# Writing down TensorE's order in the scan stage of a hybrid S5, attention and FFN step, and moving eight modulation products into it

## The chip, the cores and the metric

One NeuronCore of one Trainium2 chip runs the whole step as one program. The metric is the device time of one execution in microseconds; smaller is better. The kernel before was run three times and profiled once.

## What is computed

One layer is applied with the same weights to 128 context tokens and to 128 latent tokens (model width 2048), so that every weight matrix is multiplied with 256 token columns. Cut to what matters here:

```python
mod = silu(cond) @ w_mod + b_mod          # 12288 columns: shift1 scale1 gate1 shift2 scale2 gate2
xm  = rmsnorm(x) * (1 + scale1) + shift1
u, q, k, v, g_s, g_a = split(xm @ w_in)   # 1024, 1024, 256, 256, 2048, 2048 columns
# branch S: per group of 16 channels a 64-dim complex diagonal recurrence, forwards and backwards
h = scan(lam_bar, b_bar @ u, h0)          # one for each of the two directions
y = u * d + real(C @ h)                   # both directions added
z = gelu(y);  z = z * sigmoid(z @ w_glu)
# branch A: grouped-query attention with a sink logit
merged = sigmoid(g_s) * (z @ w_ssm_o) + sigmoid(g_a) * (attention @ w_attn_o)
x  = x + gate1 * (merged @ w_out)
xm2 = rmsnorm(x) * (1 + scale2) + shift2
x  = x + gate2 * ((silu(conv(xm2 @ w_up)_a) * conv(xm2 @ w_up)_b) @ w_down)
```

All data are fp32. The large products are made in three matmuls on a split of each operand into a rounded high part and the low rest (lo·hi, hi·lo and hi·hi); the small ones run in plain fp32.

## The kernel before

**Loads.** Weights come from DRAM in tiles of 512 KB (two rows of 128, 512 columns), one DMA each, issued by SyncE (SP) in the order of the program. They land in the pool `raw`, which has five buffers (`RAW = 5`). There are two kinds of users. A *weight chunk* of a large product is split: ScalarE (ACT) rounds it to `hi` (line 184), VectorE (DVE) takes the rest `lo` (line 185), and then its raw buffer is free; TensorE (PE) runs 24 matmuls of 128x256 on it. The split is written two chunks ahead of its use and has a raised priority. A *modulation pair* is two raw tiles which PE reads directly in one burst of four fp32 matmuls (the trace has eight rows for it, line 263); both buffers are free only when the burst has run. `burst` keeps a pair together.

**The scan stage.** The 64 groups are worked off in eight quarters `q`. For each quarter PE multiplies the channels with the input matrix (`bu_mm`, 16 fp32 matmuls), DVE rotates the result (`rot_in`, twice), runs the two scans (`scans`) and rotates back (`rot_out`, twice), and PE adds up the output (`yout`: 7 matmuls on the channels and 64 on the states), which ACT passes through gelu. Beside this stand `m_gen` (16 matmuls for the taps inside a block of four tokens), the products that prepare the matrices of a later quarter on DVE (`b_prod`, `c_prod`, `tables`), their copies on ACT, and 16 transposes on PE (`b_exp`). Transposes, the attention and the convolution's rows share one PSUM buffer, `misc`, so each user of it waits until the copy of the one before is made.

**What fills it.** While the chain of a quarter waits, PE works on 56 weight chunks (attention gate, attention output, SSM gate: the list `fill`) and on 48 modulation bursts (`modfill`, column groups 8 to 19). `weave` spreads the two lists evenly between the steps of the scan. That is the order of the program only: the framework's scheduler decides the order on each engine, by priority and its own estimate of when operands are there, and may take an instruction ahead of earlier ones. The attention's last softmaxes stand just ahead of the scan stage in the program.

**The up projection.** Column groups 20 to 23 of `w_mod` (gate2) are multiplied later: four bursts while the second norm is made, and twelve between the weight chunks of the first third of the up projection.

Of the kernel before, what the change touches and what calls it, by code (L numbers as in the profile page):

```python
# [97 lines left out]
def tile_hybrid_step(ctx, tc, a):  # L98
# [35 lines left out]
    steps = []  # L134
# [161 lines left out]
    def mod_steps(gs, pool="raw"):  # L296
        nb = len(gs)
        st = {}

        def chunk(b, ku):  # L300
            def f(raw):
                if ku % 2 == 0:
                    st["r"] = raw
                    return
                if b == 0 and ku == 1:
                    st["a"] = PS([128, 512], "mod")
                prev = None
                for i, r in ((ku, raw), (ku - 1, st["r"])):
                    for j in range(2):
                        with tc.issue_after(prev.ins) if prev is not None else nullcontext():  # L310
                            prev = mod_mm(st["a"], 2 * i + j, r[:, j, :], b, b == 0 and i < 2, b + 1 == nb and i > 5)
                if b + 1 == nb and ku == 7:
                    one = all(g == gs[0] + i for i, g in enumerate(gs))
                    mod_pp(st["a"], nb, [(4 * gs[0], 0, 4, 0, nb)] if one else [(4 * g, 0, 4, i, 1) for i, g in enumerate(gs)])
            return f
        return [Step(chunk(b, ku), wsrc(a["w_mod"], 2 * ku, 512 * MOD_AT[g]), False, pool, frees=2 * (ku % 2)) for b, g in enumerate(gs) for ku in range(8)]
# [364 lines left out]
    def weave(main, *fills):  # L681
        n = len(main)
        pos = [0] * len(fills)
        for i, s_ in enumerate(main):
            steps.append(s_)
            for k, fl in enumerate(fills):
                fl, lo, hi = fl if isinstance(fl, tuple) else (fl, 0.0, 1.0)
                while pos[k] < len(fl) and pos[k] * (hi - lo) * n < (i + 1 - lo * n) * len(fl):
                    end = burst(fl, pos[k])
                    steps.extend(fl[pos[k]:end])  # L690
                    pos[k] = end
        for k, fl in enumerate(fills):
            steps.extend((fl[0] if isinstance(fl, tuple) else fl)[pos[k]:])
# [33 lines left out]
    modfill = []  # L727
    for i in range(8, 20, 4):
        modfill += mod_steps(list(range(i, i + 4)))
    weave(ssm.stages(), (fill, FF0, FF1), (modfill, MF0, MF1))  # L730
    for i in range(NGS, 4):
        steps.extend(gs(i))

# [242 lines left out]
            gfb.append(t)  # L976

    CUT = [0, 8, 15, 22]
    g2s = mod_steps([20, 21, 22, 23])
    for x in g2s[:G2B]:  # L980
        x.pool = "first"

# [63 lines left out]
def SSM(nc, a, T4, S4, T2, PS, hp, ident, i32r, dvec, uT):  # L1046
# [241 lines left out]
    def b_prod(qd, ri):  # L1288
        if ri == 0:
            G["tB"] = S4([128, 2, 4, 8, 16], "tB")  # L1290
            G["BL"] = []
        prod(G["tB"][:, ri], "B", G["LB"], qd, 0, ri, 1, 1 - ri, OP.add if ri else OP.subtract)

    def b_exp(qd, d):
        BD, tB = G["BD"], G["tB"]
        for h in range(2):
            hs = slice(64 * h, 64 * h + 64)
            for ri in range(2):
                src = tB[hs, ri].rearrange("p k (q d) c -> p d q k c", d=2)[:, d]
                ACT(BD[hs, ri, :, :, h, :], src if d else src[:, :, ::-1, :], AF.Copy)  # L1300
                if d == 0:
                    ACT(G["B0"][hs, ri, :, h, :], tB[hs, ri, 0], AF.Copy)
        BL = S4([128, 2, 4, 128], "BL")
        G["BL"].append(BL)
        for ri in range(2):
            p = PS([128, 4, 128], "misc")
            for q in range(4):
                TR(p[:, q, :], BD[:, ri, q].rearrange("p e g c -> p (e g c)"), ident)
            ACT(BL[:, ri], p, AF.Copy)

    def u_exp(qd):
        G["U4", qd] = hp.tile([128, 4, 64], F32, tag="U4", name="U4", bufs=2)
# [133 lines left out]
    def s(f, *x):  # L1446
        return Step(lambda: f(*x))

    def b_side(q):
        if q > 7:  # L1450
            return []
        return [s(b_prod, q, 0), s(b_prod, q, 1), s(b_exp, q, 0), s(tables, q), s(b_exp, q, 1)]

    def c_side(q):
        return [s(c_prod, q, 0), s(c_prod, q, 1)] if q < 8 else []

    def first():
        return b_side(0) + c_side(0) + [s(decay, 0)]

    def stages():  # L1460
        st = [s(u_exp, 0), s(u_exp, 1), s(c_exp, 0), s(bu_mm, 0), s(rot_in, 0, 0), s(m_gen, 0), s(rot_in, 0, 1)] + b_side(1) + c_side(1)
        for q in range(8):
            st += [s(scans, q), s(rot_out, q, 0), s(rot_out, q, 1)]
            if q < 7:
                st += [s(decay, q + 1), s(bu_mm, q + 1)]
            if q < 6:
                st += [s(u_exp, q + 2)]
            st += [s(yout, q)]
            if q < 7:
                n = [s(c_exp, q + 1), s(rot_in, q + 1, 0), s(rot_in, q + 1, 1), s(m_gen, q + 1)]  # L1470
                b_, c_ = b_side(q + 2), c_side(q + 2)
                st += n[:2] + b_[:1] + n[2:3] + b_[1:2] + n[3:] + b_[2:] + c_
        st.append(Step(finals))
        return st
    S.first = first
    S.stages = stages
    return S
# [26 lines left out]
```

## Time and profile before

| | us |
|---|---|
| median of three runs | 1551.19 (1549.31 to 1555.21) |
| profiled execution | 1552.15 |
| its span in the trace | 1550.1 |
| PE busy | 1491.0 (96% of the span) |
| PE weight loads busy | 1311.1 (85%) |
| DVE busy | 1007.7 (65%) |
| ACT busy | 766.7 (49%) |

The trace covers the span; the remaining 2 us lie around it. PE's busy time counts each matmul with its modelled tail, so that a stretch in which PE waits little after each matmul looks fuller than it is. Times inside the trace are counted from the span's start.

### The profile page before, as it was taken

How to read it: one execution, taken by the hardware profiler on the slowest of the kernel's cores; microseconds unless marked ns; L12 is line 12 of the kernel's file. 1: busy time of each engine (PE TensorE's matmuls, PEld its weight loads, DVE VectorE, ACT ScalarE, POOL GpSimd, SP SyncE). 2: the span in 40 equal slices, each digit the busy share in tenths (PEclk: the TensorE clock that was granted, in tenths of full speed). 3: DMA queues.
4: the chain of work that ended last, by engine and by line, in shares of the span. 5: the costliest groups of instructions: out<-in, count | busy, mean ns of one | idle time of the engine just before them, and what ended most of it. 6: DMA issues, size and time to landing. Idle time of an engine off the chain costs nothing.

```text
span 1550.1 us, 29294 instructions
## 1 busy us (share of the span) xinstructions
PE 1491.0 (96%) x11871; PEld 1311.1 (85%) x11871; DVE 1007.7 (65%) x1541; ACT 766.7 (49%) x1191; POOL 85.7 (6%) x179
## 2 busy tenths in 40 slices
PE   6989999999899999999999999999999999999997
PEld 5758799778677788998689999889999988999986
DVE  4997776468866566765665656655665655666665
ACT  6335537645545666544554544433544543545543
POOL 2000004022321000000000000000000000000000
PEclk9999999999999999999999999999999999999999
DMA  9999754774676677975566676765555565566563
GB/s 352 352 340 321 286 196 157 258 277 156 209 241 238 240 250 274 310 244 192 172 242 235 205 245 201 238 200 190 176 192 181 181 197 191 175 205 197 170 203 123
DMA packets 104246, 349.18 MB, mean 225 GB/s; under 512 B 13900, under 2 KB 16628, under 8 KB 104112
## 3 DMA queue, kind: packets, MB, share of 16 engines
q1 hardware_dynamic: 98576, 344.20, 64.9%
q0 software_dynamic: 5312, 3.05, 0.8%
q8 instruction: 93, 1.52, 0.4%
q14 instruction: 41, 0.34, 0.1%
q10 hardware_dynamic: 224, 0.08, 0.0%
HBM read 343.76 MB, written 2.46 MB: 223 GB/s over the span
## 4 chain that ended last, share of the span: by engine, by line
PE 83%; DMA 8%; DVE 4%; ACT 2%; issue 1%; POOL 1%; SPq 0%; DVEq 0%; ACTq 0%
PE acc L395 16%; PE acc L396 16%; PE acc L397 16%; PE acc L421 8%; PE acc L422 8%; PE acc L423 8%; PE mod L263 5%; DMA raw<-in_w_mod_dram 2%; DMA raw<-in_w_in_dram 2%; PE bu L1375 1%; DVE lo L185 1%; DMA rw<-in_w_mod_dram 1%; DMA U<-u 1%; DMA raw<-in_w_attn_o_dram 1%; ACT hi L184 1%
## 5 line engine op out<-in xcount | busy, mean ns | idle before, releaser
L185 DVE TENSOR_TENSOR lo<-raw,hi 128x1024 fp32r<-128x1024 f32 (+1 forms) x456 | 538.7, 1186 | 444.8 <-ACT hi L184 442.8
L184 ACT ACTIVATE hi<-raw 128x1024 fp32r<-128x1024 f32 (+1 forms) x456 | 468.5, 1029 | 609.1 <-PE acc L397 260.7
L395 PE MATMUL acc<-yh,lo 128*128 128x256 f32 x1408 | 400.0, 284 | 0.0
L396 PE MATMUL acc<-yl,hi 128*128 128x256 f32 x1408 | 398.8, 283 | 0.0
L397 PE MATMUL acc<-yh,hi 128*128 128x256 f32 x1408 | 398.7, 283 | 0.0
L395 PEld LDWEIGHTS acc<-yh,lo 128*128 128x128 f32 x1408 | 270.3, 192 | 8.9 <-DVE lo L185 4.2
L396 PEld LDWEIGHTS acc<-yl,hi 128*128 128x128 f32 x1408 | 270.3, 192 | 0.1
L397 PEld LDWEIGHTS acc<-yh,hi 128*128 128x128 f32 x1408 | 270.2, 192 | 0.0
L395 PE MATMUL acc<-xh,lo 128*128 128x256 f32 x568 | 166.8, 294 | 9.3 <-ACT sig L672 4.8
L396 PE MATMUL acc<-xl,hi 128*128 128x256 f32 x568 | 163.4, 288 | 0.0
L397 PE MATMUL acc<-xh,hi 128*128 128x256 f32 x568 | 163.1, 287 | 0.0
L422 PE MATMUL acc<-lo,ff 128*128 128x512 f32 x352 | 136.8, 389 | 0.0
L423 PE MATMUL acc<-hi,ff 128*128 128x512 f32 x352 | 136.8, 389 | 0.0
L395 PEld LDWEIGHTS acc<-xh,lo 128*128 128x128 f32 x568 | 109.2, 192 | 31.4 <-DVE lo L185 6.9
L421 PE MATMUL acc<-hi,ff 128*128 128x512 f32 x352 | 127.8, 390 | 0.0
L396 PEld LDWEIGHTS acc<-xl,hi 128*128 128x128 f32 x568 | 109.6, 193 | 2.4 <-issue 2.2
L397 PEld LDWEIGHTS acc<-xh,hi 128*128 128x128 f32 x568 | 109.5, 193 | 0.7 <-issue 0.7
L263 PE MATMUL mod<-raw,cst 128*32 128x512 f32 x480 | 72.2, 631 | 8.0 <-DMA raw<-in_w_mod_dram 7.2
L421 PEld LDWEIGHTS acc<-hi,ff 128*128 128x128 f32 x352 | 66.1, 188 | 14.7 <-issue 1.1
L423 PEld LDWEIGHTS acc<-hi,ff 128*128 128x128 f32 x352 | 66.1, 188 | 13.7
L422 PEld LDWEIGHTS acc<-lo,ff 128*128 128x128 f32 x352 | 66.1, 188 | 13.5
L1316 POOL DMA_DIRECT2D U<-u x128 | 62.6, 497 | 159.6 <-PE bu L1375 138.5
(365 smaller groups left out, 2149.3 us busy)
## 6 DMA issues: line engine op xcount, KB each, us to landing
raw<-in_w_up_dram SPq DMA_DIRECT2D x176, 512.0 KB, 4.2
raw<-in_w_mod_dram SPq DMA_DIRECT2D x120, 512.0 KB, 5.1
raw<-in_w_in_dram SPq DMA_DIRECT2D x88, 512.0 KB, 4.5
raw<-in_w_down_dram SPq DMA_DIRECT2D x88, 512.0 KB, 4.3
rw<-in_w_mod_dram SPq DMA_DIRECT2D x56, 512.0 KB, 6.6
raw<-in_w_out_dram SPq DMA_DIRECT2D x32, 512.0 KB, 4.1
rw<-in_w_mod_first_dram SPq DMA_DIRECT2D x16, 512.0 KB, 7.4
raw<-in_w_in_dram SPq DMA_DIRECT2D x32, 256.0 KB, 6.1
```

The lines of the kernel that those rows point to most:

```text
L184: ACT(th[:, w], raws[n][:, w], AF.Copy)
L185: TT(tl[:, w], raws[n][:, w], f32(th[:, w]), OP.subtract)
L263: return MM(acc[32 * j:32 * j + 32], cst[:, kt, 6 - 2 * b:38 - 2 * b], rhs, start=start, stop=stop, skip_group_check=True, tile_position=( ...
L395: MM(o, wl, xh, start=start, stop=False, skip_group_check=True)
L396: MM(o, wh, xl, start=False, stop=False, skip_group_check=True)
L397: MM(o, wh, xh, start=False, stop=stop, skip_group_check=True)
L421: MM(accs[s], xl, hi[:, j, :], start=(kt == first), stop=False)
L422: MM(accs[s], xh, lo[:, j, :], start=False, stop=False)
L423: lastmm[0] = MM(accs[s], xh, hi[:, j, :], start=False, stop=(kt == last - 1))
L1316: nc.gpsimd.dma_start(G["U4", qd][32 * e:32 * e + 32, q, :], u[32 * q:32 * q + 32, 64 * e:64 * e + 64])
L1375: MM(bu[:, ri, x], BL[d][:, ri, q, :], u[:, :, ::-1] if d else u, start=(x == 0), stop=True, skip_group_check=True)
```

## The change

The scan stage's part of PE is put into a region in which PE keeps the order of the program (`manual_schedule`); the other engines are scheduled as before. The stage's steps are written as a period that is the same for every quarter, with places marked `F` (one weight chunk) and `M` (one modulation burst): seven `F` and six `M` for a quarter. `b_exp` is cut into its copies (`b_bd`) and its transposes (`b_tr`), and several steps stand elsewhere in the period. Column groups 20 and 21 join `modfill`, so that 56 bursts are spread over 48 places `M`; the up projection keeps groups 22 and 23.

```diff
-    weave(ssm.stages(), (fill, FF0, FF1), (modfill, MF0, MF1))
+    modfill += mod_steps([20, 21])
+    plan = ssm.stages()
+    region = ExitStack()
+    step(lambda: region.enter_context(tc.manual_schedule(engines={mybir.EngineType.PE})))
+    left = {"fill": [[u] for u in fill], "mod": []}
+    while modfill:
+        end = burst(modfill, 0)
+        left["mod"].append(modfill[:end])
+        modfill = modfill[end:]
+    share = {k: (len(v), plan.count(k)) for k, v in left.items()}
+    seen = dict.fromkeys(left, 0)
+    for x in plan:
+        if x in left:
+            seen[x] += 1
+            n, m = share[x]
+            for _ in range(n * seen[x] // m - n * (seen[x] - 1) // m):
+                steps.extend(left[x].pop(0))
+        else:
+            steps.append(x)
+    step(region.close)
+    steps.append(ssm.finals())
...
-    g2s = mod_steps([20, 21, 22, 23])
+    g2s = mod_steps([22, 23])
...
     def stages():
-        st = [s(u_exp, 0), s(u_exp, 1), s(c_exp, 0), s(bu_mm, 0), s(rot_in, 0, 0), s(m_gen, 0), s(rot_in, 0, 1)] + b_side(1) + c_side(1)
+        F, M = "fill", "mod"
+        st = [s(u_exp, 0), s(u_exp, 1), s(c_exp, 0)] + b_side(1)
         for q in range(8):
...
+            n = q + 1
+            more = n < 8
+            st += [s(bu_mm, q), s(rot_in, q, 0), M, s(rot_in, q, 1), F, s(scans, q)]
+            st += [s(decay, n)] if more else []
+            st += [M, s(m_gen, q), F, s(rot_out, q, 0), M]
+            st += [s(b_bd, n, 0)] if more else []
+            st += [s(rot_out, q, 1), F]
+            st += [s(tables, n), s(b_tr, n, 0, 0), M, s(b_tr, n, 0, 1), F] if more else [M, F]
+            st += ([s(b_bd, n, 1)] if more else []) + c_side(n) + [F]
+            st += [s(b_tr, n, 1, 0), M, s(b_tr, n, 1, 1), F] if more else [M, F]
+            st += b_side(n + 1) + [s(yout, q)]
+            st += [s(c_exp, n)] if more else []
+            st += [s(u_exp, q + 2)] if q < 6 else []
+            st += [F, M]
```

The changed kernel's instructions can be listed in the order in which each engine gets them. At the end of the attention PE had, before, the last score matmuls (L625) and the first half of an attention output (L658) with weight chunks (L395 to L397) between them, taken from the scan stage's fill:

```order
L625 MATMUL bu<-kT,pg 128x128 x3
L658 MATMUL misc<-P,pg 128x512
L658 MATMUL misc<-P,kT 128x512
L625 MATMUL bu<-kT,pg 128x128
L396 MATMUL acc<-xl,hi 128x256
L397 MATMUL acc<-xh,hi 128x256
L395 MATMUL acc<-xh,lo 128x256
```

The changed kernel has there, in one go, the transposes of probabilities (L651), the attention outputs (L658) and the first transposes for the scan (L1330, `b_tr`):

```order
L651 MATMUL misc<-kc,P 128x128 x4
L625 MATMUL bu<-kT,pg 128x128 x4
L658 MATMUL misc<-P,pg 128x512
L658 MATMUL misc<-P,kT 128x512
L625 MATMUL bu<-kT,pg 128x128 x4
L651 MATMUL misc<-kc,P 128x128 x4
L658 MATMUL misc<-P,pg 128x512
L651 MATMUL misc<-kc,P 128x128 x8
L658 MATMUL misc<-P,pg 128x512
L658 MATMUL misc<-P,kT 128x512
L1330 MATMUL misc<-kc,BD 128x128 x8
```

What PE does for the scan stage's fill can no longer move ahead of the region, so nothing stands between these any more.

On SP, the queue of the loads, this is the border of two quarters in the changed kernel (`raw<-in_w_mod_dram` x2 is one modulation pair, a row of another matrix is a weight chunk):

```order
L155 DMA raw<-in_w_mod_dram 128x1024 x2
L155 DMA raw<-in_w_in_dram 128x1024 x2
L155 DMA raw<-in_w_mod_dram 128x1024 x6
L155 DMA raw<-in_w_in_dram 128x1024
L155 DMA raw<-in_w_mod_dram 128x1024 x2
L155 DMA raw<-in_w_attn_o_dram 128x1024
```

Before, pairs and chunks alternated over the whole stage:

```order
L155 DMA raw<-in_w_mod_dram 128x1024 x2
L155 DMA raw<-in_w_attn_o_dram 128x1024
L155 DMA raw<-in_w_mod_dram 128x1024 x2
L155 DMA raw<-in_w_attn_o_dram 128x1024 x2
L155 DMA raw<-in_w_mod_dram 128x1024 x2
L155 DMA raw<-in_w_attn_o_dram 128x1024
```

The places `M` at the end of a quarter get two bursts, and with the first of the next quarter three pairs follow each other.

On DVE a quarter of the changed kernel begins like this (L185 splits a weight chunk, L1410 to L1413 are `rot_in`, L1419 the scans, L1427 to L1429 `rot_out`):

```order
L185 TENSOR_TENSOR lo<-raw,hi 128x1024
L1410 TENSOR_TENSOR vv<-bu,tab 128x512
L1412 TENSOR_TENSOR vv<-vv,t_4921 128x512
L185 TENSOR_TENSOR lo<-raw,hi 128x1024
L1413 TENSOR_TENSOR vv<-vv,keep 128x8
L1419 SCALAR_TENSOR_TENSOR vv<-R,vv 128x512 x2
L1427 TENSOR_TENSOR H<-vv,tab 128x16x32
L1429 TENSOR_TENSOR H<-H,t_5041 128x16x32
L185 TENSOR_TENSOR lo<-raw,hi 128x1024
```

The rows that repeat are left out: between the first split and the second stand six large operations of `rot_in`, between the scans and the third split five of `rot_out`. The first split is that of the first chunk of the quarter, the second and third those of the next two.

## Rows read from the trace of the kernel before

**Rows 1.** The page: busy time of each engine, share of the span, instructions.
```profile
PE 1491.0 (96%) x11871; PEld 1311.1 (85%) x11871; DVE 1007.7 (65%) x1541; ACT 766.7 (49%) x1191; POOL 85.7 (6%) x179
```

**Rows 2.** Stretches: length, busy PE, PEld, DVE, ACT, POOL, PE's clock, DMA share, GB/s.
```profile
350.00:400.00 50.00, 44.05 (x613) 36.57 (x611) 44.37 (x80) 32.48 (x79) 15.63 (x32) 0.93 0.38 130
400.00:450.00 50.00, 48.28 (x512) 38.47 (x513) 35.41 (x55) 25.51 (x53) 7.83 (x16) 1.00 0.77 261
610.00:700.00 90.00, 90.00 (x667) 86.23 (x666) 59.25 (x68) 45.34 (x52) 0.99 (x2) 1.00 0.82 282
850.00:900.00 50.00, 50.00 (x414) 47.09 (x413) 29.18 (x36) 23.54 (x29) 0.00 (x0) 1.00 0.68 238
```

**Rows 3.** SP's waits in the scan stage: total us, times, longest.
```profile
SPq L155 <- PE mod L263: 101.2, 33, 18.4
```

**Rows 4.** PE in order of time where the two orders part, and where the stage ends.
```profile
259.77 1.04 PE L263 MATMUL mod<-raw,cst 128*32 128x512 f32 x2
...
608.62 0.36 PE L395 MATMUL acc<-zh,lo 128*128 128x256 f32 x1
```

**Rows 5.** ACT and DVE in order of time at the attention's end.
```profile
265.70 0.61 ACT L652 ACTIVATE P<-misc 128x512 f32<-128x512 f32 x1
...
278.47 1.28 ACT L638 ACT_TABLE_LOAD   x1 [1.85 <-DVE st L633]
...
282.27 0.40 ACT L638 ACTIVATE P<-bu,st 128x128 f32<-128x128 f32 x1
...
286.59 1.25 ACT L1328 ACTIVATE CL<-bct 64x128 f32<-64x128 f32 x4
...
303.13 0.83 ACT L1300 ACTIVATE BD<-tB 64x256 f32<-64x256 f32 x2
...
297.96 0.69 DVE L664 TENSOR_TENSOR ol<-misc,oh 128x512 fp32r<-128x512 f32 x1
```

**Rows 6.** The chain that ended last: start, length of the piece, engine, tile, line, count.
```profile
294.34 1.72 PE misc L658 x4
...
316.93 0.12 PE acc L397
...
319.21 0.44 PE misc L1308 x4
319.65 1.73 PE bu L1375 x16
...
342.56 1.51 PE y L1416 x14
...
520.14 0.73 PE y L1338 x32
...
546.27 1.94 PE y L1425 x128
```

**Rows 7.** The same chain around two loads that a finished modulation burst let start.
```profile
308.45 1.02 PE mod L263 x8
309.47 4.14 DMA raw<-in_w_attn_o_dram
...
314.79 1.24 DVE lo L185
316.07 0.39 PE acc L395
...
396.63 0.29 SPq L155
396.97 4.28 DMA raw<-in_w_attn_o_dram
```

**Rows 8.** The chain again, on DVE: one large operation of `rot_in`, one scan.
```profile
386.68 0.60 DVE t L1389
...
392.18 1.11 DVE vv L1397
```

**Rows 9.** The chain in the up projection: one modulation burst.
```profile
831.85 1.00 PE mod L263 x8
```

More of the change, by code (lines that the diff above doesn't have):

```diff
@@ L1290, in b_prod, with b_bd @@
             G["tB"] = S4([128, 2, 4, 8, 16], "tB")
-            G["BL"] = []
         prod(G["tB"][:, ri], "B", G["LB"], qd, 0, ri, 1, 1 - ri, OP.add if ri else OP.subtract)
-    def b_exp(qd, d):
+    def b_bd(qd, d):
         BD, tB = G["BD"], G["tB"]
@@ L1302, in b_exp, with b_tr @@
                     ACT(G["B0"][hs, ri, :, h, :], tB[hs, ri, 0], AF.Copy)
[L1303 to L1309, printed above, removed]
+    def b_tr(qd, d, ri):
+        if (d, ri) == (0, 0):
+            G["BL"] = []
+        if ri == 0:
+            G["BL"].append(S4([128, 2, 4, 128], "BL"))
+        p = PS([128, 4, 128], "misc")
+        for q in range(4):
+            TR(p[:, q, :], G["BD"][:, ri, q].rearrange("p e g c -> p (e g c)"), ident)
+        ACT(G["BL"][d][:, ri], p, AF.Copy)
     def u_exp(qd):
@@ L1447, in s, with b_side @@
         return Step(lambda: f(*x))
[L1449 to L1452, printed above, removed]
     def c_side(q):
         return [s(c_prod, q, 0), s(c_prod, q, 1)] if q < 8 else []
+    def b_side(q):
+        return [s(b_prod, q, 0), s(b_prod, q, 1)] if q < 8 else []
     def first():
-        return b_side(0) + c_side(0) + [s(decay, 0)]
+        n = b_side(0) + [s(b_bd, 0, 0), s(b_tr, 0, 0, 0), s(b_tr, 0, 0, 1), s(tables, 0), s(b_bd, 0, 1), s(b_tr, 0, 1, 0), s(b_tr, 0, 1, 1)]
+        return n + c_side(0) + [s(decay, 0)]
     def stages():
-        st = [s(u_exp, 0), s(u_exp, 1), s(c_exp, 0), s(bu_mm, 0), s(rot_in, 0, 0), s(m_gen, 0), s(rot_in, 0, 1)] + b_side(1) + c_side(1)
+        F, M = "fill", "mod"
+        st = [s(u_exp, 0), s(u_exp, 1), s(c_exp, 0)] + b_side(1)
         for q in range(8):
[L1463 to L1473, printed above, removed]
+            n = q + 1
[12 more added lines that the diff above has]
+            st += [F, M]
         return st
+    S.finals = lambda: s(finals)
     S.first = first
```

## The prediction

> **What bounds the kernel now.** The page comes first: PE is busy for 96% of the span, every other engine far less [rows 1]. So time is saved only where PE waits, or where PE gets less work. The view by stretches shows where that is: after the scan stage PE has no gap at all (90.00 of 90 us, 50.00 of 50 us in the up projection), while in the scan stage it lost 5.95 us of one stretch of 50 us and 1.72 us of the next [rows 2]. These are lower bounds, since a busy PE includes the tails of matmuls. Counting work by prices is stricter. The chain gives them: 0.12 us for a matmul of a weight chunk, so 2.87 us for its 24; 0.44 us for four transposes; 1.73 us for 16 rows of `bu_mm`, which has 32, so 3.45; 1.51 for `yout`'s product with the channels, 1.94 for its product with the states, 0.73 for `m_gen` [rows 6], and 1.0 us for a modulation burst [rows 7]. A quarter with seven chunks and six bursts is then 20.1 + 6.0 + 3.45 + 0.73 + 1.76 + 1.51 + 1.94 = 35.5 us of PE work, eight of them 284 us. With 12 us for the attention's remainder and an earlier chunk, PE had some 296 us to do between the place where the two orders part, 259.8, and the first matmul of the gated unit at 608.6 [rows 4]. That stretch took 348.8 us, so PE lost about 53 us in it.
>
> What it waits for is seen in SP's queue and in the chain. SP waited 101.2 us in this stage for modulation bursts to free a buffer [rows 3], and the chain passes through loads that such a burst let start: burst over at 309.47, load 4.14 us, rounding, rest, first matmul of the chunk at 316.07 [rows 7]. So from the end of a burst to the chunk that needed its buffer there are 6.6 us. Five buffers are short, and a burst holds two until PE has run it.
>
> **What the change does, part by part.** *Eight bursts leave the up projection.* There PE has no gap [rows 2], each burst is 1.0 us on the chain [rows 9], and no other engine is near its limit. I take 8.0 us, with 0.6 for the waits and switches around them: minus 8.6 us. If something else set the pace there, it would be nothing; that is the other end.
>
> *Eight bursts enter the scan stage*: a quarter's PE work becomes 36.5 us, the same 8 us in sum. The 16 loads come along, on the same SP queue.
>
> *The attention's end loses its cover.* Before, PE filled the waits of the last softmaxes with nine chunks and five bursts from the scan stage, by the order of its instructions, so 31 us of work. The region forbids that. What is left is a chain through one PSUM buffer, worked out from the end of an ACT copy at 266.3 [rows 5]: attention output 1.7 [rows 6], then on ACT a split, a table load and a sigmoid, its own copy 0.6 and DVE's rest 0.69, to 270.9; the last maxima on DVE, an estimated 1.0, to 271.9; copy 0.6, table load and eight exponentials 4.2 (from 278.47 to 282.67 in [rows 5]), to 276.7; copy 0.6, eight copies into `BD` and `B0`, 2.6, and those into `CL`, 1.25 [rows 5], all of which ACT has ahead of the next copy out of `misc`, to 281.2; two rounds of transposes and copy, the last output with its evacuation, to 285.9; four rounds of 0.44 us transposes and 0.6 us copy, with a pair of `BD` copies of 0.83 us and two rows of the convolution between, to 292.2; the rest of `bu_mm`, 1.7. The first burst of the region starts near 294.0. Of these 34 us PE works some 18; it loses 16 that it did not lose before. If ACT's copies fall better it is 288; if the rows of the convolution come late, 297.
>
> *The period.* Here the written order meets the five buffers. At a quarter's border two bursts end the old quarter, `bu_mm` (3.45 us) and one burst begin the new, and then comes the first chunk. Of these pairs four buffers are held, so the second tile of the third pair and the first chunk's load are issued only when the first of the two bursts is over. Let the second end at 0. The loads are issued from -1.0, the chunk's behind the other; 6.6 us from a burst's end to the matmul [rows 7], or 7.0 by the other load in that group (0.34 to its start, 4.28 for itself, then rounding and rest), give 5.6 to 6.0. I take 6.5, with half a microsecond for standing second. PE could have been there at 4.45.
>
> Next, DVE. Its order has the first chunk's split ahead of `rot_in`, and the third chunk's split behind `rot_in`, the second split, the scans and five operations of `rot_out`. At 0.60 us for a large operation, 1.11 for a scan [rows 8] and 1.24 for a split [rows 7]: 3.6 + 1.2 + 2.3 + 3.0 + 0.4 for small ones + 1.2 = 11.7 us after the first split, so the third chunk starts near 18.2. By its own work PE would be there at 12.95 (3.45, a burst, a chunk, a burst, `m_gen`, a chunk, a burst). That is 5.2 us lost per quarter. Behind it DVE runs ahead again, and I find no further wait of size; half a microsecond goes to copies out of `misc` and to the sigmoids' evacuations. So a quarter takes 36.5 + 5.2 + 0.5 = 42.2 us. Bounds: 38.7 if the first chunk's load came early and only DVE's chain counted (`bu_mm` over at 3.45, the third chunk at 15.2, 2.2 us lost), 44 if splits also queue behind one DVE operation each.
>
> *The rest.* `yout` of the last quarter now has a chunk and two bursts behind it that cover gelu and the split of `z`; before, the gated unit followed without a gap too, so this is worth nothing. But the two bursts hold four buffers, and the second load of `w_glu` pays 3 us. POOL's copies of the channels are issued a quarter ahead and stay off the path.
>
> **The sum.** First quarter, with its chunks already split and its `bu_mm` counted: 34.5. Then seven of 42.2, minus 1.8 for the transposes that the last has no more, plus 3: 294.0 + 34.5 + 295.4 - 1.8 + 3 = 625.1, against 608.6: plus 16.5. With minus 8.6 it is plus 7.9 us. Against the profiled execution, 1552.15, that is 1560; the median of the runs is 1 us lower, so **1559 us**, 0.5% more. I take half a per cent, 7.8 us, for what a measurement of this kernel can tell from no change: the forecast lies on that edge.
>
> **The clock.** The granted clock was 0.93 in one of these stretches and 1.00 in the next, though PE waited in both [rows 2]; 0.93 of 50 us is 7 us at 1.2 GHz instead of 2.4, up to 3.5 us lost. The sum holds nothing for it. Beside this stands a rule of the Trainium skill ("TensorE: Matmul & The Clock Gate", section on HAM oscillation): a wait for data that recurs with every tile throttles the engine anew each time, and half of the throttled time is lost. By that rule each quarter's wait would cost clock as well as time; the trace shows it in some stretches and not in others.
>
> **Rivals.**
> *The order flows (faster).* Place: the border of quarters. If the first chunk's load took a buffer freed by an earlier burst, a quarter would be 38.7 us: 294.0 + 34.5 + 270.9 - 1.8 + 3 = 600.6, minus 8.0, and with the up projection minus 16.6: 1535. For it: before, PE lost about as much per quarter to `gelu`, `BD` copies and sigmoids, and the written period sets all of these far apart. Against: the row of six modulation loads in SP's order, and 101.2 us of waits for bursts. It decides at 41.1 us per quarter: below, the change gains; 40.0 would be 0.5%.
> *Nothing to see (same).* A quarter of 41 and a bare stretch that ends at 291: minus 3 and minus 8 from my sum, 1548. Everything within 1543 and 1559 belongs here.
> *The clock falls in every quarter (slower still).* 3.5 us for each of seven: plus 24, 1583; in half of them 1571.
> *The up projection gives nothing back.* Then 1568. Its full PE speaks against it.
> *The written order changes nothing* can't be: the two orders differ on PE over the whole stage.
>
> **How the numbers follow.** Slower as summed, or because the up projection gives nothing back, 0.34; slower by the clock 0.08; within half a per cent 0.31; the order flows 0.27. The forecast is the sum, 1559; its own range goes from 1549 to 1570 by the bounds of the bare stretch (-6, +3) and of a quarter (a microsecond each way, so 7). The range for 8 in 10 must reach the fast case: 1533 to 1574; 0.1 is left below and 0.1 above.
>
> **What would show it.** In the changed kernel: PE mostly idle from about 266 to 294, with the rows of `misc` one behind the other; each pair of scans some 42 us behind the one before; PE's first chunk after each `bu_mm` waiting for `lo`, and the third one again; the gated unit starting near 625; the up projection 8 to 9 us shorter. The forecast is wrong if the quarters are at 39 or less (load or DVE chain misjudged), if the bare stretch is shorter than 28 us, or if the clock falls to 1.2 GHz in every quarter.

## The result

| | kernel before | changed kernel |
|---|---|---|
| median of four runs (us) | 1552.33 (1549.31 to 1555.21) | 1605.63 (1601.51 to 1614.19) |
| ratio, 95% interval | | 1.0351 [1.0302, 1.0399] |
| profiled execution (us) | 1552.15 | 1601.51 |
| its span, PE's granted clock | 1550.1, 0.990 | 1599.4, 0.976 |

3.5% slower. The forecast was 1559 with a range up to 1574: the direction was right, the size was not. In the profiled executions it is 1601.5 against 1560, so 41.5 us are missing from the sum.

### The profile page after: what moved, and what is told of

Read it like the earlier page. It is cut to its first block, busy times and chain, and to the rows that moved or that the text cites. A ratio compares the mean times of both kernels' runs of the same rounds, so it can differ in the third digit from the quotient of the medians.

```text
span 1599.4 us, 29312 instructions
## 1 busy us (share of the span) xinstructions
PE 1499.5 (94%) x11879; PEld 1324.1 (83%) x11879; DVE 1002.0 (63%) x1543; ACT 767.9 (48%) x1190; POOL 85.9 (5%) x179
## 4 chain that ended last, share of the span: by engine, by line
PE 69%; DMA 6%; DVE 3%; ACT 2%; issue 1%; SPq 0%; DVEq 0%; ACTq 0%
PE acc L395 14%; PE acc L396 14%; PE acc L397 14%; PE acc L421 7%; PE acc L422 7%; PE acc L423 7%; DMA raw<-in_w_in_dram 4%; PE mod L263 2%; DMA raw<-in_w_attn_o_dram 2%; DVE lo L185 1%; ACT hi L184 1%; PE y L1447 1%; PE bu L1397 1%; PE misc L1330 1%; PE y L1438 1%
## 5 line engine op out<-in xcount | busy, mean ns | idle before, releaser
L185 DVE TENSOR_TENSOR lo<-raw,hi 128x1024 fp32r<-128x1024 f32 (+1 forms) x456 | 537.8, 1185 | 498.7 <-ACT hi L184 494.6
L395 PE MATMUL acc<-yh,lo 128*128 128x256 f32 x1408 | 399.1, 284 | 0.0
L397 PE MATMUL acc<-yh,hi 128*128 128x256 f32 x1408 | 398.8, 283 | 0.0
L395 PEld LDWEIGHTS acc<-yh,lo 128*128 128x128 f32 x1408 | 270.4, 192 | 2.6 <-issue 1.7
L397 PEld LDWEIGHTS acc<-yh,hi 128*128 128x128 f32 x1408 | 270.3, 192 | 0.0
L395 PE MATMUL acc<-xh,lo 128*128 128x256 f32 x568 | 170.1, 299 | 22.2 <-DVE lo L185 22.1
L397 PE MATMUL acc<-xh,hi 128*128 128x256 f32 x568 | 165.5, 292 | 0.0
L395 PEld LDWEIGHTS acc<-xh,lo 128*128 128x128 f32 x568 | 112.8, 199 | 40.5 <-DVE lo L185 29.9
L396 PEld LDWEIGHTS acc<-xl,hi 128*128 128x128 f32 x568 | 112.8, 199 | 1.9 <-issue 1.7
L397 PEld LDWEIGHTS acc<-xh,hi 128*128 128x128 f32 x568 | 112.7, 199 | 0.2 <-issue 0.2
L423 PEld LDWEIGHTS acc<-hi,ff 128*128 128x128 f32 x352 | 66.1, 188 | 13.7
L422 PEld LDWEIGHTS acc<-lo,ff 128*128 128x128 f32 x352 | 66.1, 188 | 13.6
L923 ACT ACTIVATE ab<-acc,cw 128x256 f32<-128x256 f32 x88 | 46.9, 558 | 42.0 <-DVE ab L925 32.7
```

The costliest lines, as they stand in the source:

```text
L185: TT(tl[:, w], raws[n][:, w], f32(th[:, w]), OP.subtract)
L395: MM(o, wl, xh, start=start, stop=False, skip_group_check=True)
L396: MM(o, wh, xl, start=False, stop=False, skip_group_check=True)
L397: MM(o, wh, xh, start=False, stop=stop, skip_group_check=True)
L422: MM(accs[s], xh, lo[:, j, :], start=False, stop=False)
L423: lastmm[0] = MM(accs[s], xh, hi[:, j, :], start=False, stop=(kt == last - 1))
```

## The profile after

The page's line of busy time, which answers to [rows 1]:

```profile
PE 1499.5 (94%) x11879; PEld 1324.1 (83%) x11879; DVE 1002.0 (63%) x1543; ACT 767.9 (48%) x1190; POOL 85.9 (5%) x179
```

PE has the same work (and eight small matmuls for one more group's end) in a span that is 49 us longer. The view by stretches shows the whole stage, cut at the first burst of the region, at each quarter's first `bu_mm` and at the gated unit (columns as in [rows 2]: length, five engines, PE's clock, DMA share, GB/s):

```profile
259.80:302.70 42.90, 26.86 (x129) 19.40 (x128) 23.12 (x50) 28.20 (x69) 3.27 (x6) 0.75 0.12 39
302.70:345.50 42.80, 39.17 (x417) 31.81 (x416) 23.75 (x41) 19.87 (x42) 7.84 (x16) 0.85 0.55 188
345.50:388.50 43.00, 38.00 (x451) 31.12 (x447) 27.13 (x44) 24.82 (x49) 7.84 (x16) 1.00 0.72 260
388.50:438.20 49.70, 41.56 (x458) 34.20 (x454) 29.07 (x48) 21.10 (x46) 7.83 (x16) 0.93 0.64 226
438.20:481.90 43.70, 39.41 (x451) 32.65 (x447) 26.97 (x44) 21.04 (x44) 7.86 (x16) 0.96 0.72 256
481.90:531.30 49.40, 40.88 (x458) 34.09 (x454) 26.65 (x44) 24.09 (x47) 7.85 (x16) 0.93 0.65 227
531.30:575.40 44.10, 37.94 (x450) 31.13 (x446) 25.78 (x42) 24.78 (x49) 7.84 (x16) 1.00 0.73 254
575.40:622.70 47.30, 39.94 (x458) 32.68 (x454) 23.18 (x39) 23.69 (x46) 0.00 (x0) 0.96 0.68 243
622.70:667.10 44.40, 38.40 (x436) 30.86 (x432) 19.81 (x28) 13.81 (x21) 3.07 (x6) 0.96 0.69 249
667.10:760.00 92.90, 92.04 (x682) 87.80 (x683) 63.03 (x71) 45.81 (x52) 0.00 (x0) 1.00 0.86 297
```

Three things are to be seen. The attention's end and the first quarter ran at a granted clock of 0.75 and 0.85. The quarters alternate between 43 to 44 us and 47 to 50. And from 667.1 on next to nothing is lost (PE is busy for 92.04 of 92.90 us), as before. Set against the steps of the sum:

| step | forecast | measured | off by |
|---|---|---|---|
| 259.8 to the first burst of the region | 34.2 | 42.9 | 8.7 |
| first quarter from there | 34.5 | 42.8 | 8.3 |
| the other seven, with the end | 296.6 | 321.6 | 25.0 |
| from the gated unit to the end, change to before | -8.6 | -9.2 | -0.6 |

The last row is 1599.4 - 667.1 = 932.3 against 1550.1 - 608.6 = 941.5.

What PE waited for between 260 and 670 (view of the waits: engine, tile, line, what it waited for, total us, times, longest):

```profile
PE acc L395 <- DVE lo L185: 27.6, 17, 2.5
PE misc L1330 <- ACT BL L1331: 12.2, 10, 3.6
PE mod L272 <- DVE macc L268: 9.3, 3, 4.9
PE misc L651 <- DVE P L643: 5.6, 1, 5.6
```

The first line is weight chunks waiting for their split, about twice a quarter; the third is the end of a group of modulation columns, three times: once in each of the three quarters of 47 to 50 us. SP, over the stage from 309, answers to [rows 3]:

```profile
SPq L155 <- PE mod L263: 176.8, 43, 10.3
```

101.2 us had become 176.8. The transfers themselves had room: a quarter at full clock moved 254 to 260 GB/s, the stretch behind 667.1 moved 297. One quarter followed on PE (start, us, engine, line, operation; in brackets the idle time before it and its releaser):

```profile
344.51 1.04 PE L263 MATMUL mod<-raw,cst 128*32 128x512 f32 x8
345.48 3.79 PE L1397 MATMUL bu<-U,BL 128*128 128x64 f32 x32
349.19 1.07 PE L263 MATMUL mod<-raw,cst 128*32 128x512 f32 x8
351.88 0.39 PE L395 MATMUL acc<-xh,lo 128*128 128x256 f32 x1 [1.62 <-DVE lo L185]
...
354.93 1.06 PE L263 MATMUL mod<-raw,cst 128*32 128x512 f32 x8
...
360.22 1.07 PE L263 MATMUL mod<-raw,cst 128*32 128x512 f32 x8
363.80 0.39 PE L395 MATMUL acc<-oh,lo 128*128 128x256 f32 x1 [2.51 <-DVE lo L185]
```

The border's second burst ends at 345.48; the first chunk comes 6.4 us later (forecast 6.5), the third at 18.3 (18.2), and this quarter, at full clock, takes 43.0 (42.2). That looks like the forecast period to the tenth. But the third chunk's split says otherwise. SP, ACT and DVE around it:

```profile
356.02 0.33 SPq L155 DMA_DIRECT2D raw<-in_w_attn_o_dram  x1
```
```profile
360.24 1.06 ACT L184 ACTIVATE hi<-raw 128x1024 fp32r<-128x1024 f32 x1 [0.17 <-DMA raw<-in_w_attn_o_dram]
```
```profile
362.53 1.21 DVE L185 TENSOR_TENSOR lo<-raw,hi 128x1024 fp32r<-128x1024 f32 x1
```

Its load is issued at 356.02, when the burst that PE began at 354.93 is over, and lands at 360.24; rounded at 361.30, it stands 1.2 us behind `rot_out` on DVE. So the load alone would have had PE waiting till 362.6, DVE's chain added the last 1.2.

## The experiments

All were timed against the kernel before; the fifth column is the start of the gated unit in the profiled execution (608.6 before, 667.1 changed kernel).

| run | median, us | before in the same series | ratio [95%] | gated unit |
|---|---|---|---|---|
| e1_move_only | 1565.4 | 1549.9 | 1.0105 [1.0073, 1.0137] | 633.2 |
| e2_order_only | 1588.7 | 1549.9 | 1.0261 [1.0221, 1.0301] | 640.7 |
| e3_free | 1560.3 | 1549.9 | 1.0060 [1.0038, 1.0083] | 621.2 |
| e4_cover | 1574.1 | 1549.9 | 1.0147 [1.0104, 1.0190] | 643.3 |
| e5_spread | 1598.4 | 1551.8 | 1.0284 [1.0237, 1.0332] | 668.1 |
| e8_free48 | 1555.2 | 1551.8 | 1.0016 [0.9993, 1.0039] | 608.4 |
| e9_dummy | 1611.6 | 1551.8 | 1.0384 [1.0337, 1.0431] | 675.2 |
| e10_mpp | 1607.7 | 1551.8 | 1.0358 [1.0316, 1.0400] | 667.5 |
| e11_no_loads | 1552.1 | 1556.4 | 0.9978 [0.9963, 0.9994] | 618.9 |
| e12_no_scan | 1617.6 | 1556.4 | 1.0396 [1.0364, 1.0427] | 676.6 |
| e13_cover48 | 1582.2 | 1556.4 | 1.0179 [1.0146, 1.0213] | 629.4 |
| e14_keep | 1607.6 | 1556.4 | 1.0331 [1.0302, 1.0360] | 669.2 |
| e15_five | 1608.8 | 1555.7 | 1.0345 [1.0316, 1.0375] | 673.6 |
| e15_six | 1583.5 | 1555.7 | 1.0176 [1.0151, 1.0202] | 642.2 |
| e16_no_mod_loads | 1559.3 | 1555.7 | 1.0023 [1.0010, 1.0035] | 625.1 |
| e17_free_six | 1551.1 | 1555.7 | 0.9977 [0.9961, 0.9992] | 608.9 |
| e18_cover_six | 1575.5 | 1554.8 | 1.0147 [1.0128, 1.0167] | 634.8 |
| e18_free48_six | 1551.9 | 1554.8 | 0.9975 [0.9955, 0.9996] | 595.5 |

Not all came out as one of their theories had it: e1 and e5 fell between the ranges of theirs, e12, e13 and e18_cover_six were slower than any range named, e16 was faster than any, and e2 and e4 lie a microsecond below theirs.

### The change in its parts

The move alone, in the old order:

```diff
+    modfill += mod_steps([20, 21])
...
-    g2s = mod_steps([20, 21, 22, 23])
+    g2s = mod_steps([22, 23])
```

> The scan stage of the kernel before, order left to the scheduler, with column groups 20 and 21 moved into it; 16 loads and eight bursts more there, eight bursts fewer in the up projection. Theory W (the written order loses the time, through PE's waits): the eight bursts find room between waits, the up projection gives back 9 us, so 1543 to 1555 us. Theory L (the scan stage has no room for 16 more loads through five buffers, whatever the order): each pair costs a wait of some 3 to 6 us, so 1575 us or more.

The written order alone is the changed kernel without these lines.

> The written order with 48 bursts, one at each place, so that no two follow each other at a quarter's end; groups 20 to 23 stay in the up projection. Theory W: the bare end of the attention and the waits inside the quarters stay, only the doubled burst goes: 1590 to 1606 us, first burst of the region again near 302 in the trace. Theory L: most of the loss goes with the loads: 1575 us or less.

The new program with PE scheduled freely is the changed kernel without the line that opens the region, with 56 bursts and then with 48:

```diff
-    step(lambda: region.enter_context(tc.manual_schedule(engines={mybir.EngineType.PE})))
```

> The changed program, its period and its 56 bursts, but PE's order left to the scheduler. Theory W: PE's chunks move ahead into the attention's end again and waits inside the quarters are filled: 1550 to 1570 us. Theory P (the new place of the steps in the period, and with it the order on DVE and ACT, loses the time, not PE's fixed order): 1590 us or more.

> The changed program and period, PE's order left to the scheduler, and groups 20 to 23 back in the up projection (48 bursts). If the moved product costs in any order, as in the kernel before (8 us of work and 16 of waiting for 9 given back): 1540 to 1552 us, faster than the same program with 56 bursts (1560). If the new period has room for them: the same 1555 to 1562.

The order costs 38.8 us, the move 15.5; together 54.3, the change 53.3: two losses that add up. The new program itself costs nothing that shows (e8). With the same program and the same bursts, fixing PE's order makes the difference between +0.6% and +3.5%. And the move is no even trade: e1 gets its 9 us back behind the gated unit (932.7) and pays 24.6 for 8 us of work in the stage.

### The attention's end and the clock

```diff
+    for i in range(9):
+        steps.append(fill.pop(0))
+        if i % 2 == 0:
+            end = burst(modfill, 0)
+            steps.extend(modfill[:end])
+            del modfill[:end]
     plan = ssm.stages()
```

> The changed kernel with nine weight chunks and five bursts taken out of the region and put ahead of it, where the scheduler may use them at the attention's end; the rest of the written order stays. If the bare end with its falling clock is half of the loss (Theory W's first part): 1575 to 1585 us, granted clock 1.00 from 260 to 300. If the time is only put off, since the loads or the scan's own chain then set the pace: 1598 us or more.

24.2 us over the kernel before instead of 53.3: the lost cover is worth 29 us. PE's stretch is now filled, at full clock:

```profile
259.80:300.00 40.20, 39.94 (x296) 32.72 (x295) 26.63 (x48) 29.80 (x64) 1.49 (x2) 1.00 0.55 196
```

Useless matmuls in place of the cover, to tell the clock from the missing work:

```diff
...
+        for _ in range(240):
+            MM(p[:, 0:NT], XH[0][:, 0, 0:128], XH[1][:, 0, :], start=True, stop=True, skip_group_check=True)
...
```

> The changed kernel with 240 matmuls of 128x256 on data that is already there, written to a bank that nobody reads, put ahead of the region: 29 us of extra PE work that helps nothing and that the scheduler can spread over the bare end of the attention. If half of the miss there is the clock that falls to 1.2 GHz while PE is idle: granted clock 1.00 from 260 to 345, first burst of the region some 5 to 8 us earlier, the first quarter 8 us shorter, 1588 to 1596 us although PE does more. If the bare end costs by its missing work alone: 1604 to 1612 us.

The total lies in the range named for "missing work alone", but it can't decide: the matmuls got ahead of the softmaxes' chain in PE's order, and the first burst came at 312.5, 9.8 us later. What they do show is the first quarter from there on. At a clock of 0.95 instead of 0.85 it takes 38.7 us, not 42.8; 3.2 of these 4.1 us are PE's busy time (35.98 for 39.17), the rest is waiting:

```profile
312.50:351.20 38.70, 35.98 (x417) 28.62 (x416) 24.25 (x42) 20.50 (x44) 7.84 (x16) 0.95 0.57 209
```

The same idea inside the quarters, 18 useless matmuls ahead of each third chunk:

```diff
...
-            st += [s(rot_out, q, 1), F]
+            st += [s(rot_out, q, 1), "busy", F]
```

> The changed kernel with 18 useless 128x256 matmuls (2.15 us of PE work at 0.12) in every quarter just ahead of the third chunk, where PE waits about 2.3 us for its split. Theory A, the half-speed stretches inside the quarters follow from these waits and cost time of their own: with the wait filled, the clock in 345:667 is 1.00 almost throughout (0.96 before), and the time falls by 3 to 10 us, to 1596 to 1602. Theory B, the waits cost only their own length: no change (1604 to 1607). If PE does not wait there in most quarters: plus 10 to 17.

No change, though 17 us of PE work were added: PE had been waiting there for that long. The clock of the quarters stayed at 0.96 (346.2 to 669.2). So filling this wait buys no clock, and theory A fell for the third chunk's wait. It did not fall for waits as such, as the changed kernel's trace shows. From 388.5 to 667.1 the clock falls to half seven times, near 404, 424, 445, 489, 510, 595 and 636. Each fall begins in a wait of PE of 1.7 to 4.9 us or within two microseconds of its end, and only the one at 595 belongs to a third chunk; the others stand at first or second chunks, at groups' ends and at a copy of the transposes. Six other waits of 1.4 to 2.5 us in these quarters have no fall behind them. The first of the seven, behind the wait that ends at 402.45 (its row stands under "The ends of the groups"):

```profile
404.10:407.40 3.30, 3.30 (x18) 3.30 (x17) 3.30 (x6) 1.90 (x7) 0.00 (x0) 0.50 0.28 107
```

### What the chunks wait for

The crowd of three pairs at the border was the forecast's reason for the first chunk. Here the seventh burst stands earlier and no pair is doubled:

```diff
-            st += ([s(b_bd, n, 1)] if more else []) + c_side(n) + [F]
+            st += ([s(b_bd, n, 1)] if more else []) + c_side(n) + [F, M]
```

> The changed kernel with one more place M in each quarter (behind the chunk that follows c_side), so that each place gets one burst and none is doubled at a quarter's end; same 56 bursts, same loads, PE's order written. If the crowd of three pairs at the border makes PE wait for the loads and starts the scan's chain late: each quarter 2 to 3 us shorter, 1585 to 1592 us. If only the number of loads counts, or the clock: 1600 us or more.

The first chunk's wait is gone in the quarter shown, and little is won (+2.8%): the third chunk still waits 2.28 us.

```profile
355.19 1.07 PE L263 MATMUL mod<-raw,cst 128*32 128x512 f32 x8
359.97 1.07 PE L263 MATMUL mod<-raw,cst 128*32 128x512 f32 x8
363.31 0.39 PE L395 MATMUL acc<-oh,lo 128*128 128x256 f32 x1 [2.28 <-DVE lo L185]
```

At that point DVE's chain, as forecast, seemed the answer. So the scans were left out:

```diff
-            st += [s(bu_mm, q), s(rot_in, q, 0), M, s(rot_in, q, 1), F, s(scans, q)]
+            st += [s(bu_mm, q), s(rot_in, q, 0), M, s(rot_in, q, 1), F]
```

> The changed kernel with the two scans of each quarter left out (the states are then wrong), everything else in place. Theory A, the third chunk waits for its split behind DVE's chain (rotation, scans, rotation back): the chain is 2.2 us shorter, the third chunk starts near 16 instead of 18.3 us after the quarter's bu_mm starts, a quarter is 2 us shorter, eight of them give 16 to 19 us: some 1588. Theory B, loads set the third chunk: no change, 1604 to 1607.

Nothing was gained; the ratio is 0.4% above that of the changed kernel, at a clock of 0.94 in the seven quarters for 0.96. In the quarter that begins at 348.65, SP, ACT, DVE and PE have:

```profile
361.42 0.33 SPq L155 DMA_DIRECT2D raw<-in_w_attn_o_dram  x1
```
```profile
365.94 1.06 ACT L184 ACTIVATE hi<-raw 128x1024 fp32r<-128x1024 f32 x1 [2.67 <-DMA raw<-in_w_attn_o_dram]
```
```profile
367.03 1.23 DVE L185 TENSOR_TENSOR lo<-raw,hi 128x1024 fp32r<-128x1024 f32 x1 [1.72 <-ACT hi L184]
```
```profile
368.31 0.38 PE L395 MATMUL acc<-oh,lo 128*128 128x256 f32 x1 [2.14 <-DVE lo L185]
```

DVE now waits for ACT, ACT for the load, and the load was let go by a burst that ended at 361.2: 7.1 us from there to the matmul, during which PE has only `m_gen`, a chunk and a burst to do (0.8 + 3.1 + 1.0). The third chunk itself comes later than in the changed kernel, 19.7 us after the quarter's start for 18.3: the first chunk starts 0.7 us later and takes 1.5 us longer, at a clock of 0.63 (355.7 to 360.3), and the burst stands behind it. Such a wait can arise wherever bursts and chunks alternate: with five buffers the tile five loads earlier is that of the burst two places back.

One buffer more is the direct test. A tile takes 4 KB of each partition; two smaller pools gave up 3 KB for it. The control has the smaller pools alone.

```diff
-RAW, HL, W4, NS4, W2, LOADS = 5, 3, 18, 5, 3, 5
+RAW, HL, W4, NS4, W2, LOADS = 6, 3, 18, 5, 2, 5
...
-        G["U4", qd] = hp.tile([128, 4, 64], F32, tag="U4", name="U4", bufs=2)
+        G["U4", qd] = hp.tile([128, 4, 64], F32, tag="U4", name="U4", bufs=1)
```

> Control for the next run: the changed kernel with five raw buffers as it is, but with two instead of three small work buffers (2 KB) and one instead of two for the channels of a quarter, which is what makes room for a sixth raw buffer. All theories: 1602 to 1610, as the changed kernel, if those buffers are no limit.

> The same with six raw buffers. Theory L: the third chunk of a quarter and the first wait for loads that the burst two places before lets start; with a sixth buffer the third chunk's load hangs on the first chunk's split instead and is early, the first chunk's load no longer stands behind another: 2 to 3 us per quarter, 15 to 24 in all, 1580 to 1590. Theory J, load and DVE's chain end within 1.2 us of each other at the third chunk, so that taking away either moves it little: 4 to 9 us in all, 1596 to 1601, with the third chunk still some 18 us after the start of bu_mm. Theory D, DVE's chain alone: 0 to 2 us.

25.3 us less than the control: theory L's number. In the quarter that begins at 339.97 the first chunk comes 5.4 us later, the third 15.9:

```profile
345.34 0.39 PE L395 MATMUL acc<-xh,lo 128*128 128x256 f32 x1 [0.58 <-DVE lo L185]
...
355.90 0.39 PE L395 MATMUL acc<-oh,lo 128*128 128x256 f32 x1 [1.65 <-DVE lo L185]
```

Over the seven quarters PE waited 32.0 us (302.2 less 270.2 busy), in the control 49.7 (329.1 less 279.4); the clock was 0.98 for 0.94. So some 9 of the 27 us are busy time, at the higher clock. What is left of the third chunk's wait is now DVE's: its tile is rounded at 353.33, and the split stands in DVE's queue until 354.62.

```profile
352.27 1.06 ACT L184 ACTIVATE hi<-raw 128x1024 fp32r<-128x1024 f32 x1 [0.62 <-DMA raw<-in_w_attn_o_dram]
```
```profile
354.62 1.22 DVE L185 TENSOR_TENSOR lo<-raw,hi 128x1024 fp32r<-128x1024 f32 x1
```

Last, the region with none of its modulation loads, all bursts in place:

```diff
...
+    left["mod"] = [[resident(k)] for k in range(len(left["mod"]))]
```

> The changed kernel in which all 56 bursts of the region multiply a tile that lies in SBUF, so PE's work and order are the same and 112 of the region's 168 loads are gone; the modulation columns of these groups are then wrong. Theory J: the waits for the first and third chunks shrink to what DVE's chain leaves; an undisturbed quarter is 38.7 to 40 us instead of 43 to 44, the ends of the groups still wait for DVE: 25 to 40 us less, 1565 to 1580. Theory D, the chain of DVE and ACT sets the quarters, not the loads: less than 8 us.

```profile
344.50:382.80 38.30, 37.80 (x450) 31.14 (x446) 26.95 (x44) 24.46 (x49) 7.81 (x16) 1.00 0.33 101
382.80:423.20 40.40, 38.12 (x459) 31.15 (x455) 29.12 (x48) 22.24 (x47) 7.81 (x16) 1.00 0.32 96
423.20:461.50 38.30, 37.80 (x451) 31.15 (x447) 26.95 (x44) 20.69 (x44) 7.81 (x16) 1.00 0.33 101
461.50:501.60 40.10, 37.99 (x459) 31.29 (x455) 26.56 (x44) 23.19 (x46) 7.82 (x16) 1.00 0.32 97
```

Same work and same order on PE: 38.3 us for a plain quarter, 40.1 to 40.4 with a group's end, full clock in these four, and from 344.5 to the gated unit 280.6 us instead of 321.6. PE waits for no split any more: it reaches the third chunk 13.6 us after the start of `bu_mm` and finds it there. DVE has the same scans, rotations and splits, but not in the same order. The third chunk's split stands behind one operation of `rot_out`, where the changed kernel had five:

```profile
354.41 0.67 DVE L1444 TENSOR_TENSOR H<-vv,tab 128x512 f32<-128x512 f32 x1
354.99 1.22 DVE L185 TENSOR_TENSOR lo<-raw,hi 128x1024 fp32r<-128x1024 f32 x1
```

The program is one reason: a split is written two tiles of the load list ahead of its use (not two chunks, as "The kernel before" has it), and a modulation pair counts as two tiles. Without the pairs two tiles are two chunks, so the splits stand earlier. This run thus takes away the loads and eases DVE's queue, and does not say how much of the 41 us each is worth. The sixth buffer leaves the written place of the splits alone: it shows the loads as the first limit, and DVE's queue as the next one behind them.

### The ends of the groups

> The changed kernel with the small matmuls that end each modulation group (on DVE's transpose of the sums) one weight chunk later in the written order. If PE stands in front of them while DVE, busy with its own queue, has not yet made the transpose (about 5 us in each of two quarters, 1 or 2 in a third): 1594 to 1600 us. If the chunk behind them would have waited anyway: 1603 us or more.

The small matmuls that end a group were put one chunk later, behind the transpose they wait for. No gain. Their own waits are gone, but at the first group's end PE then waits for DVE to read the sums, before the next group's first burst may overwrite them:

```profile
412.51 1.72 PE L263 MATMUL mod<-raw,cst 128*32 128x512 f32 x8 [4.00 <-DVE modp L284]
```

Around the group's end at 398.8 the changed kernel's ACT, DVE and PE have:

```profile
398.27 1.06 ACT L184 ACTIVATE hi<-raw 128x1024 fp32r<-128x1024 f32 x1 [4.75 <-DMA raw<-in_w_attn_o_dram]
```
```profile
399.36 1.23 DVE L185 TENSOR_TENSOR lo<-raw,hi 128x1024 fp32r<-128x1024 f32 x1 [0.90 <-ACT hi L184]
...
401.71 0.69 DVE L268 STREAM_TRANSPOSE macc<-mod 128x512 f32<-128x512 f32 x1
```
```profile
402.45 0.27 PE L272 MATMUL mod<-macc,kc 128*32 128x32 f32 x8 [3.49 <-DVE macc L268]
```

The transpose stands in DVE's queue behind a split and one scan (1.22 us, left out above), and the split waits 0.90 us, through ACT, for a load. So the shortage of loads has a part in it, and DVE's own work ahead of the transpose the larger one here. Without modulation loads, and with DVE's queue eased, a group's end costs 2 us in the two quarters shown, instead of 5 to 6.

### What the move costs

The move alone again, but the eight moved bursts multiply a tile that lies in SBUF:

```diff
-    modfill += mod_steps([20, 21])
+    modfill += [resident(k) for k in range(8)]
```

> The move alone (old order of PE, eight more bursts in the scan stage), but the eight moved bursts multiply a tile that is already in SBUF, so the stage has eight microseconds more PE work and not one load more; the modulation columns of groups 20 and 21 are then wrong. The move alone cost 15.5 us: 24.6 in the stage for 8 us of work, 9 given back. Theory A, the stage is held up by its loads through five buffers: the bursts without loads cost their 8 to 10 us of PE work or less, where PE waits anyway, and with 9 given back the time is that of the kernel before, 1551 plus or minus 3. Theory B, the extra comes from PE's work and the scheduler's order with it: as with loads, some 1565.

Minus 0.2% instead of plus 1.05%: moved without its loads the work loses nothing, so the 16 loads are what the move costs. Theory A held. (As in e16, the splits beside these bursts are also written earlier; what that is worth was not taken apart.)

### Can a version win?

> The written order with 48 bursts (nothing moved from the up projection) and with nine chunks and five bursts put ahead of the region, where the scheduler may use them as the attention's cover. If the parts add up, order +38.8, cover -31.5: 1557 to 1560 (+0.4 to +0.6%). If the cover is worth less without the moved bursts: 1565 to 1570. If a written order can beat the free one once it has its cover: under 1548.

> The written order with 56 bursts, with nine chunks and five bursts ahead of the region as the attention's cover and with six raw buffers. Cover (minus 31.5) and the sixth buffer (minus 25) would bring the changed kernel from 1606 to 1549 if they add up, so to the kernel before or a little below. If they take away the same waits: 1560 to 1570.

> The new program and 56 bursts with PE scheduled freely (1560.3 with five buffers, 0.6% above the kernel before) and with six raw buffers and the smaller work buffers. If the loads of the moved bursts are what kept it above the kernel before: 1545 to 1555, so the same or up to 0.4% faster. If not: 1558 to 1563.

> The new program with PE scheduled freely, 48 bursts (nothing moved) and six raw buffers: tells whether the 0.2% of the free version with 56 bursts and six buffers comes from the buffer alone (then 1550 here too) or from the moved bursts that the buffer makes room for (then 1555 to 1560 here, where loads are less of a limit).

The gains of the written order's remedies do not add up, and both forecasts for them were too low: cover and 48 bursts leave 1.8%, cover and six buffers 1.5%, as cover alone. In e18_cover_six the splits' waits fall from 25.0 to 10.4 us against e4_cover, but those for ACT's copies of the transposes rise from 10.9 to 17.5: in a fixed order PE stands at the next late operand. What else holds it back was not taken apart. The free order with six buffers is 0.2% faster than the kernel before, and as fast with 48 bursts as with 56, so the buffer did that and not the move. It is the only version below the kernel before that does all the work, and by less than the half per cent set as the bound. The kernel before with six buffers was not run.

## Why the prediction was wrong

**Right.** Direction; the up projection's gain (-9.2 for -8.6); the lost cover as a place of loss; first and third chunk of an undisturbed quarter waiting, and its 43 to 44 us for 42.2. The rivals "the order flows" and "nothing to see" fell with them.

**The clock taken as nothing.** This is the step that failed most: "The sum holds nothing for it." By the prediction's own working (a stretch at 0.93 of 50 us loses up to 3.5) the loss is at most (1 - clock) times length. That gives up to 10.7 us in the bare stretch, 6.4 in the first quarter and 12.4 in the five later quarters below 1.00, together at most 29.5 of the 41.5.

*In the bare stretch* the waits came out as forecast, 16.0 us for 16. PE's own work was off: 26.9 us busy where 18 were counted, at a clock of 0.75. The 32 rows of `bu_mm` alone took 6.9 us there for 3.45. With the cover the clock was 1.00.

*In the first quarter* PE was busy for 39.2 us, where the sum had 34.5 for everything, at 0.85. The rest is a wait for a copy of the transposes, 3.6 us long (the longest of the second line of waits), where the sum had half a microsecond. e9 took 3.2 us of busy time off.

*In the other seven* the waits too are nearly as forecast in sum, 45.5 us for 42.9. PE was busy for 276.1 us (the table's seven rows), where the sum had 253.7. Up to 12.4 of these 22.4 us are clock. The rest is work priced too low: 36.5 us a quarter, where a quarter at full clock shows 38.0 busy and lasts 38.3 in e16, in which PE hardly waits.

The rival that put the clock into every quarter was nearer in time, 1583. In these seven it was half right, five of seven and up to 12.4 us for 24, and it had nothing for the stretch and the quarter ahead of them. A rule of the Trainium skill ("TensorE: Matmul & The Clock Gate", section on HAM oscillation) has a data wait that recurs with every tile throttle the engine each time, in a kernel whose work on a tile is shorter than the wait for the next. The prediction left that condition out. Here PE was busy for 38 of 43 us, and the trace agrees in part: seven falls stand at waits, none stands in 345.5 to 388.5 with its two waits of 1.6 and 2.5 us, and e14_keep, which filled one of them, got no clock back.

**The period: right number, half the wrong reason.** The step "Next, DVE" failed as the only account of the third chunk. It put the chunk at 18.2 by DVE's queue, and that chain had its size (11.9 us from the end of the first split to the end of the third, for 11.7). But the load ends within 1.2 us of the same point, and the runs decide for the load as the first limit: leaving out the scans gained nothing, one buffer 25 us, no modulation loads (with DVE's queue eased) 41 us of the seven quarters. DVE's chain also starts on a load: it begins with the first chunk's split. That the two ends met at 18.3 is luck. The forecast applied the buffers' rule to the border's crowd alone, and e5 showed that the crowd isn't needed.

**The ends of the groups, not in the sum.** Three long quarters, with some 5 us more each than their neighbours, make about 15 of the 25 us. About 7 of these are busy time (40.8 us on average for 38.4), with five of the seven falls of the clock; the rest are waits, 9.3 us of them at the groups' ends themselves.

**The move taken as 8 for 8.6.** "The 16 loads come along, on the same SP queue" was said and priced at nothing. In the old order they cost 15.5 us net.

**The range.** The forecast's own range, 1549 to 1570, does not follow from its bounds, which add up to 1546 to 1569; no bound in it was for the clock.

**Open.** Why six buffers give part of the gain back behind the gated unit (940.6 us from there to the end, 933.7 with five), what limits the written order once it has cover and buffer, and why some waits bring the clock down and others of the same length do not.

## What to carry to other kernels

Where PE reads its operand straight from the load buffers, the price of moved work is its loads: count for each load which earlier user's end frees its buffer, and how much work PE has between that end and the use. Here this was 7 us against 5 at the third chunk of a quarter. When two chains end within a microsecond at one point, a forecast that fits does not say which of them it is; remove each by itself before believing it. A forecast that adds waits to a fully busy engine should also price what those waits do to its clock: here they were right in sum, and the clock was not in it. And a fixed order for one engine gives up the filling of gaps that a scheduler did for free, at the region's edge above all.

## What the runs showed of the hardware

The granted clock did not come back at once when PE was busy again. In the changed kernel PE had no gap from 296.2 on, half of the time with `bu_mm`, and still ran at 0.51 until 308.7. Then it ran at full clock until the wait of 3.6 us that ends at 323.4, in which it fell again:

```profile
296.20:308.70 12.50, 12.50 (x60) 10.72 (x60) 8.75 (x17) 4.34 (x9) 5.67 (x12) 0.51 0.26 87
322.00:329.00 7.00, 5.58 (x26) 5.58 (x27) 4.12 (x5) 4.55 (x8) 0.00 (x0) 0.51 0.73 259
```

In e16_no_mod_loads it fell late in the stage as well: PE was busy for 10.35 of 13.7 us ahead of 582.0 at full clock, and then without a gap, again half of the time with `bu_mm`, yet at 1.2 GHz:

```profile
568.30:582.00 13.70, 10.35 (x206) 8.91 (x208) 3.46 (x5) 9.88 (x18) 0.00 (x0) 1.00 0.25 79
582.00:595.70 13.70, 13.70 (x64) 10.62 (x57) 5.28 (x10) 0.00 (x0) 0.00 (x0) 0.50 0.13 39
```

What set its return there, no run shows.
